# Attention's first scores behind its first gate's products, and the identity matrix on SyncE's queue

## The chip, the cores and the metric

One core of a Trainium2 chip runs the kernel. The metric is device time in microseconds (us) of one execution, the median of several. TensorE (PE in the profile) multiplies matrices; VectorE (DVE), ScalarE (ACT) and GpSimd (POOL) work element by element; SyncE (SP) issues DMAs, and so does ScalarE's queue here.

## The reference, cut to what matters

One decoder layer over 512 tokens of width 1024, in float32. A normalised input h is projected; one part of the columns goes through a gated linear recurrence (HGRN2, 8 heads), another through attention with low-rank queries and keys (MLA, 8 heads); both are gated, projected, merged and added to the input.

```python
h = rms_norm(x, norm_g[l])
proj = h @ w_in[l]
hq, hf, hi, hz, cq, ckv, kr, mz, glog = jnp.split(proj, pts, axis=-1)
y_a = hgrn2_branch(hq, hf, hi, hz, lower_bounds[l], hg_norm_g[l])
y_b = mla_branch(cq, ckv, kr, mz, q_a_g[l], w_uq[l], kv_a_g[l], w_ukv[l])
...
# in mla_branch, per block of 128 queries and per head:
s = (einsum(qn, k_nope) + einsum(qp, k_pe)) * scale      # nope part, rope part
p = softmax(where(causal, s, -inf))
out = p @ v                                              # then out * silu(mz)
```

## The kernel before

Every float32 product is made of three: each operand is split into a high and a low part (`w_hi`, `w_lo`, `hT0`, `hT1`), and `mm3` issues high x high, high x low and low x high (lines 90 to 92). Activations stand as 128 channels x 512 tokens. `load_w` (from line 94) brings a tile of weights of up to 128x1024 by SyncE's queue, casts it on ScalarE (L111) and subtracts on VectorE (L112). The pools for raw, high and low tiles hold three, four and four of them, so a cast waits until TensorE has used the tile four loads before. PSUM has eight banks: three for projections (`mm_ps`) and five for the rest (`ax_ps`), both used in rotation.

The stages: a start that normalises and transposes the four token tiles of x and makes the low-rank columns; then four pairs of HGRN2 heads (`hg_pair`); then the MLA heads 0 to 7; then the merge and the output projection. A scheduler sets the order on each engine by a time line of its own. It leaves alone what is written in a `manual_schedule` block, for the engines named there. There are three such blocks. The first is the start, by hand on TensorE, ScalarE and VectorE. The third is at the last MLA head. The second, `last_outputs`, is for TensorE alone: it is the seam between the last HGRN2 pair and the first MLA head. Instructions of other parts may still be put between those of the block, but theirs keep their order.

What stands in this second block:

- `outs(scores())`: the outputs of the last two HGRN2 heads (L508 to L529);
- `mla_scores(0, ...)`, from line 654: head 0's scores, for four blocks of 128 queries with 128, 256, 384 and 512 keys; per block three products of the nope part (`kn`, `qn`; L90 to L92) and two of the rope part (`kpe`, `qp`; L664). Softmax follows on VectorE (mask L667, maximum L668, scaling L669, reciprocal L671), ScalarE (exponential L670) and GpSimd (L672);
- `mla_gate(0)`, from line 644: 24 products of 512 columns with h (`hT`), then ScalarE (L548) and VectorE (L549);
- `gated(on)`: transposes of the HGRN2 outputs (L543), then VectorE (L544). These outputs, `k_2481` and `k_2502`, come from L535, for which ScalarE squares (L533) and GpSimd takes a power (L158, L159).

The rope operand `qp` has a long way: `mla_rope(0)` copies a projection on ScalarE (L605), moves its rows by DMAs on ScalarE's queue (L607), multiplies and adds on GpSimd (L608 to L610), moves rows again (L614), casts (L616, L619) and subtracts on VectorE (L620).

Behind the block come head 1's nope projections (`mla_nope(1)`, 15 products with `cT`), the values of heads 0 to 3 (`mla_values(0)`, 6 products for each of four token tiles), and the transposes of head 0's probabilities (L685).

At the start, SyncE's queue issues x's first token tile in two halves (L198), the first weights `c_raw[0]` (L201), x's second tile, the second weights, x's other tiles, then small rows and tables. ScalarE's queue issues a gain row (L204) and the identity matrix `ident` (L205, 64 KB). `ident` is the operand of all transposes, first of those of the first token tile (L253), from the normalised tile that VectorE makes (`xn`, L245). VectorE then casts the first weights (L232) and takes their low parts (L236), and TensorE multiplies (L264).

Of the kernel before, what the change touches and what calls it, by code (L numbers as in the profile page):

```python
# [38 lines left out]
def hybrid_layer(ctx: ExitStack, tc: tile.TileContext, a):  # L39
    nc = tc.nc  # L40
# [12 lines left out]
    def mm_tile():  # L53
        return mm.tile([P, 512], F32, tag="mm", name="mm_ps")

    def ax_tile():
        return ax.tile([P, 512], F32, tag="ax", name="ax_ps")

    def z_tile():
        return zpool.tile([P, S], F32, tag="z", name="z")  # L60
# [26 lines left out]
    def mm3(ps, l, r, lsl, rsl, start, stop):  # L87

        (lh, ll), (rh, rl) = l, r
        nc.tensor.matmul(ps, lh[lsl], rh[rsl], start=start, stop=False)  # L90
        nc.tensor.matmul(ps, lh[lsl], rl[rsl], start=False, stop=False)  # L91
        nc.tensor.matmul(ps, ll[lsl], rh[rsl], start=False, stop=stop)  # L92

    def load_w(*pieces, lo_eng=None):

        raw = wraw.tile([P, WCH], F32, tag="raw", name="w_raw")
        hi = whi.tile([P, WCH], F32R, tag="hi", name="w_hi")
        lo = wlo.tile([P, WCH], F32R, tag="lo", name="w_lo")
        views, o = [], 0
        for src in pieces:  # L100
            n = int(np.prod(src.shape[1:]))
            if len(src.shape) == 4:
                _, k, h, c = src.shape
                dst = raw[:, o : o + n].rearrange("p (k h c) -> p k h c", k=k, h=h)
                for i in range(k):
                    nc.sync.dma_start(dst[:, i], src[:, i])
            else:
                nc.sync.dma_start(raw[:, o : o + n].rearrange("p (k c) -> p k c", k=src.shape[1]), src)
            views.append([t[:, o : o + n].rearrange("p (k c) -> p k c", k=src.shape[1]) for t in (hi, lo)])
            o += n  # L110
        nc.scalar.copy(hi[:, :o], raw[:, :o])  # L111
        (lo_eng or nc.vector).tensor_tensor(lo[:, :o], raw[:, :o], hi[:, :o].bitcast(F32), op=ALU.subtract)  # L112
        return views[0] if len(views) == 1 else views
# [56 lines left out]
    ident = const.tile([P, P], F32, name="ident")  # L170
# [29 lines left out]
    def load_c(kh):  # L200
        nc.sync.dma_start(c_raw[kh][:].rearrange("p (k c) -> p k c", k=4), w_c0[:, 4 * kh : 4 * kh + 4, :])  # L201

    load_x(0, 2)
    nc.scalar.dma_start(ng_row[0:33:32, :], a["norm_g"].rearrange("l (n c) -> (l n) c", n=2))  # L204
    nc.scalar.dma_start(ident[:], a["c_ident"])  # L205
    load_c(0)
    load_x(1)
    load_c(1)
# [337 lines left out]
    def silu2(z, pz):  # L546

        nc.scalar.activation(z, pz, AF.Tanh, scale=0.5)  # L548
        nc.vector.scalar_tensor_tensor(z, z, 1.0, pz, op0=ALU.add, op1=ALU.mult)  # L549
# [3 lines left out]
    def hg_pair(pair, before_gate=None, last=None):  # L553
        cc, hs = pair * 256, (2 * pair, 2 * pair + 1)
        pf = proj_ch(w_in, COL_F + cc, hT)
        kk = [hg_forget(h, pf[i]) for i, h in enumerate(hs)]
        def gate():
            pz = proj_ch(w_in, COL_ZA + cc, hT)
            zz = [z_tile() for _ in hs]
            for i in range(2):  # L560
                silu2(zz[i][:], pz[i][:])
            return zz

        if pair % 2 == 0:
            for t in range(NT):
                v_sb[t] = hw.tile([P, 512], F32, f"v{t}")
            proj_tok(w_in, COL_I + cc, hT, lambda t, ps: nc.scalar.copy(v_sb[t][:], ps[:]))
        else:
            zz = gate()
        pq = proj_ch(w_in, COL_Q + cc, hT)  # L570
        qq = [hg_query(h, pq[i], kk[i][0]) for i, h in enumerate(hs)]
        sts = [hg_states(h, kk[i][5], kk[i][1], v_sb) for i, h in enumerate(hs)]
        if before_gate:
            before_gate()
        if pair % 2 == 0:
            zz = gate()
        def scores():
            return [hg_scores(h, kk[i][2], kk[i][3], kk[i][4], qq[i][0], qq[i][1]) for i, h in enumerate(hs)]

        def outs(aa):  # L580
            return [hg_out(h, aa[i], sts[i], qq[i][2], v_sb) for i, h in enumerate(hs)]

        def gated(on):
            for i, h in enumerate(hs):
                hg_gate(h, on[i], zz[i])

        if last:
            return last(scores, outs, gated)
        gated(outs(scores()))
# [54 lines left out]
    def mla_gate(h):  # L644
        w = load_w(w_in[:, COL_ZB + h * P : COL_ZB + h * P + P].rearrange("(k p) c -> p k c", p=P))
        ps = mm_tile()
        for k in range(KD):
            mm3(ps[:], w, hT, (slice(None), k), (slice(None), k), k == 0, k == KD - 1)
        z = z_tile()
        silu2(z[:], ps[:])  # L650
        return z


    def mla_scores(h, pool, qn, kn, qp, final=False):

        pn = []
        for i in range(NT):
            n = (i + 1) * P
            bl = slice(i * P, n)
            sps = ax_tile()  # L660
            qh = qp[h % 2]
            mm3(sps[:, :n], qn, kn, (slice(None), bl), (slice(None), slice(0, n)), True, False)
            for x in range(2):
                nc.tensor.matmul(sps[:, :n], qh[:, bl], kpe[x][:, :n], start=False, stop=x == 1)  # L664
            sm = pool.tile([P, 4], F32, "sm", 4)
            p = pool.tile([P, n], F32, f"p{i}")
            nc.vector.tensor_tensor(sps[:, bl], sps[:, bl], mask_inf[:], op=ALU.add)  # L667
            nc.vector.tensor_reduce(sm[:, 0:1], sps[:, :n], axis=AX.X, op=ALU.max, negate=True)  # L668
            nc.vector.tensor_scalar(sm[:, 1:2], sm[:, 0:1], SCALE, None, op0=ALU.mult)  # L669
            nc.scalar.activation(p[:, :n], sps[:, :n], AF.Exp, scale=SCALE, bias=sm[:, 1:2], accum_out=sm[:, 2:3])  # L670
            nc.vector.reciprocal(sm[:, 3:4], sm[:, 2:3])  # L671
            (nc.vector if final else nc.gpsimd).tensor_scalar(p[:, :n], p[:, :n], sm[:, 3:4], 0.5, op0=ALU.mult, op1=ALU.mult)  # L672
            pn.append(p)
        return pn
# [41 lines left out]
    def last_outputs(scores, outs, gated):  # L716

        with tc.manual_schedule(engines={mybir.EngineType.PE}):
            on = outs(scores())
            early.append(mla_scores(0, ma_pool, *early[1], early[0]))  # L720
            z = mla_gate(0)
            gated(on)
        return z

    z = hg_pair(H // 2 - 1, first_scores, last_outputs)
    hw.close()

# [5 lines left out]
    for h in range(H):  # L733
# [6 lines left out]
        if h:  # L740
            z = mla_gate(h)
# [144 lines left out]
```

## Time and profile before

| | |
|---|---|
| time, median of 3 runs | 636.34 us (635.45 to 636.77) |
| the profiled execution | 636.65 us, its span 634.9 us |
| TensorE busy | 622.2 us, 98% of the span |
| VectorE, ScalarE, GpSimd busy | 353.0, 239.7 and 114.5 us |
| mean granted clock of TensorE | 0.995 |
| moved by DMA | 59.75 MB, mean 94 GB/s |

How to read it: the span runs from the first instruction to the last; all times inside are from its start. A row of the timeline gives start, length, engine, line, operation, and what it writes and reads, and in brackets the idle time ahead of it and what ended that. The instructions of a busy engine start a little before the one ahead has ended in these rows, since matmuls are pipelined and their ends are modelled; starts are the better measure of what one costs in a row. The granted clock is the share of full speed that the chip lets TensorE run at. A busy share near 1 does not say that TensorE is at full speed: at half the clock it is busy too.

### The profile page before, as it was taken

The page shows a single profiled execution, that of the slowest core. Times are in us where ns is not written, and L with a number is a line of the kernel's source. Part 1 is how long each engine was busy: PE and PEld are TensorE (multiplying, and loading weights), DVE is VectorE, ACT ScalarE, POOL GpSimd, SP SyncE. Part 2 cuts the span into 40 slices and gives each one's busy share as a digit, 9 for nine tenths or more (in the row PEclk, how much of TensorE's full clock was granted, in tenths as well). Part 3 has the DMA queues.
Part 4 walks back from the last instruction along what each step waited for, and adds up shares of the span by engine and source line. Part 5 has one row for each costly group of instructions (what it writes and reads, how often), then busy time and mean ns, then how long its engine had stood idle before and what let it go on. Part 6 is the DMA issues. An engine that isn't in the chain of part 4 may idle for free.

```text
span 634.9 us, 8391 instructions
## 1 busy us (share of the span) xinstructions
PE 622.2 (98%) x3204; PEld 524.1 (83%) x3204; DVE 353.0 (56%) x552; ACT 239.7 (38%) x451; POOL 114.5 (18%) x213
## 2 busy tenths in 40 slices
PE   7999999999999999989999999999999999999995
PEld 4998888888888888878888888888888888888884
DVE  7727855397954458757366758584232342434244
ACT  5554242323233232356345546383222232323223
POOL 3106200322311033321314140000000010111011
PEclk9999999999999999989999999999999999999999
DMA  7425153124115203401532232223333323324403
GB/s 234 151 66 181 47 166 90 43 67 132 35 44 146 58 21 88 116 17 35 141 96 72 55 116 84 68 66 100 99 100 99 99 69 107 102 90 162 170 14 120
DMA packets 58808, 59.75 MB, mean 94 GB/s; under 512 B 5736, under 2 KB 52238, under 8 KB 58768
## 3 DMA queue, kind: packets, MB, share of 16 engines
q1 hardware_dynamic: 56492, 55.54, 29.0%
q10 hardware_dynamic: 2132, 3.15, 1.6%
q8 instruction: 25, 0.41, 0.3%
q0 software_dynamic: 144, 0.52, 0.2%
q14 instruction: 15, 0.12, 0.1%
HBM read 55.01 MB, written 2.10 MB: 90 GB/s over the span
## 4 chain that ended last, share of the span: by engine, by line
PE 94%; DMA 2%; DVE 1%; ACT 1%; POOL 1%; ACTq 0%; issue 0%; SPq 0%; POOLq 0%
PE mm_ps L90 26%; PE mm_ps L91 26%; PE mm_ps L92 26%; PE ax_ps L91 2%; PE ax_ps L90 2%; PE ax_ps L92 2%; PE ax_ps L664 2%; PE mm_ps L264 1%; PE ax_ps L685 1%; DMA w_raw<-w_in 1%; PE ax_ps L508 1%; PE ax_ps L527 1%; PE ax_ps L529 1%; PE ax_ps L496 1%; PE ax_ps L516 1%; PE ax_ps L543 1%
## 5 line engine op out<-in xcount | busy, mean ns | idle before, releaser
L112 DVE TENSOR_TENSOR w_lo<-w_raw,w_hi 128x1024 fp32r<-128x1024 f32 (+3 forms) x90 | 108.6, 1211 | 123.0 <-ACT w_hi L111 121.3
L111 ACT CAST w_hi<-w_raw 128x1024 fp32r<-128x1024 f32 (+3 forms) x90 | 89.4, 995 | 167.3 <-PE mm_ps L91 124.0
L90 PE MATMUL mm_ps<-hT,w_hi 128*128 128x512 f32 x384 | 150.8, 393 | 0.0
L91 PE MATMUL mm_ps<-hT,w_hi 128*128 128x512 f32 x384 | 150.0, 391 | 0.0
L92 PE MATMUL mm_ps<-hT,w_lo 128*128 128x512 f32 x384 | 149.8, 392 | 0.0
L92 PEld LDWEIGHTS mm_ps<-hT,w_lo 128*128 128x128 f32 x384 | 72.1, 188 | 14.7
L90 PEld LDWEIGHTS mm_ps<-hT,w_hi 128*128 128x128 f32 x384 | 72.1, 188 | 14.4
L91 PEld LDWEIGHTS mm_ps<-hT,w_hi 128*128 128x128 f32 x384 | 72.2, 188 | 14.3
L787 POOL TENSOR_TENSOR ma<-ma,z 128x512 f32<-128x512 f32 x8 | 11.8, 1479 | 177.1 <-DVE z L786 177.1
L91 PE MATMUL mm_ps<-w_lo,hT 128*128 128x512 f32 (+1 forms) x96 | 36.5, 382 | 0.0
L92 PE MATMUL mm_ps<-w_hi,hT 128*128 128x512 f32 (+1 forms) x96 | 36.4, 382 | 0.0
L90 PE MATMUL mm_ps<-w_hi,hT 128*128 128x512 f32 (+1 forms) x96 | 36.4, 386 | 0.0
L672 POOL TENSOR_SCALAR p<-p,sm 128x128 f32<-128x128 f32 (+3 forms) x28 | 15.3, 548 | 79.4 <-DVE sm L671 47.5
L453 DVE RECIPROCAL tf<-pr 128x512 f32<-128x512 f32 x8 | 26.8, 3350 | 0.2
L670 ACT ACTIVATE p<-ax_ps,sm 128x128 f32<-128x128 f32 (+3 forms) x32 | 16.9, 529 | 24.6 <-DVE sm L669 20.9
L91 PE MATMUL mm_ps<-ya,w_hi 128*128 128x512 f32 x64 | 25.0, 390 | 0.0
L92 PE MATMUL mm_ps<-ya,w_lo 128*128 128x512 f32 x64 | 24.9, 389 | 0.0
L90 PE MATMUL mm_ps<-yb,w_hi 128*128 128x512 f32 x64 | 24.9, 389 | 0.0
L91 PE MATMUL mm_ps<-yb,w_hi 128*128 128x512 f32 x64 | 24.9, 389 | 0.0
L92 PE MATMUL mm_ps<-yb,w_lo 128*128 128x512 f32 x64 | 24.9, 389 | 0.0
L90 PE MATMUL mm_ps<-ya,w_hi 128*128 128x512 f32 x64 | 24.8, 389 | 0.0
L154 DVE TENSOR_TENSOR wo<-wo_raw,wo 128x1024 fp32r<-128x1024 f32 x8 | 9.6, 1223 | 25.9 <-ACT wo L153 25.9
(226 smaller groups left out, 1126.3 us busy)
## 6 DMA issues: line engine op xcount, KB each, us to landing
w_raw<-w_in SPq DMA_DIRECT2D x58, 512.0 KB, 3.8
w_raw<-w_proj_a SPq DMA_DIRECT2D x8, 512.0 KB, 3.4
w_raw<-w_proj_b SPq DMA_DIRECT2D x8, 512.0 KB, 3.4
wo_raw<-w_out SPq DMA_DIRECT2D x8, 512.0 KB, 3.7
xr<-x SPq DMA_DIRECT2D x4, 512.0 KB, 7.2
w_raw<-w_in SPq DMA_DIRECT2D x4, 448.0 KB, 4.8
x<-x SPq DMA_DIRECT2D x3, 512.0 KB, 9.4
w_raw<-w_uq SPq DMA_DIRECT2D x8, 192.0 KB, 2.6
```

The source lines that it names most:

```text
L90: nc.tensor.matmul(ps, lh[lsl], rh[rsl], start=start, stop=False)
L91: nc.tensor.matmul(ps, lh[lsl], rl[rsl], start=False, stop=False)
L92: nc.tensor.matmul(ps, ll[lsl], rh[rsl], start=False, stop=stop)
L111: nc.scalar.copy(hi[:, :o], raw[:, :o])
L112: (lo_eng or nc.vector).tensor_tensor(lo[:, :o], raw[:, :o], hi[:, :o].bitcast(F32), op=ALU.subtract)
L154: nc.vector.tensor_tensor(lo, src, hi.bitcast(F32), op=ALU.subtract)
L264: nc.tensor.matmul(ps, hT[l][:, 4 * kh + k, t * P : t * P + P], c_hl[kh][r][:, k * 256 : k * 256 + 256], start=kh == 0 and kind == 0 and k ...
L453: nc.vector.reciprocal(rp[:], pr[:])
L664: nc.tensor.matmul(sps[:, :n], qh[:, bl], kpe[x][:, :n], start=False, stop=x == 1)
L670: nc.scalar.activation(p[:, :n], sps[:, :n], AF.Exp, scale=SCALE, bias=sm[:, 1:2], accum_out=sm[:, 2:3])
L672: (nc.vector if final else nc.gpsimd).tensor_scalar(p[:, :n], p[:, :n], sm[:, 3:4], 0.5, op0=ALU.mult, op1=ALU.mult)
L787: nc.gpsimd.tensor_tensor(ma[:, j], ma[:, j], g[:], op=ALU.add)
```

## The change

Two edits.

```diff
     load_x(0, 2)
     nc.scalar.dma_start(ng_row[0:33:32, :], a["norm_g"].rearrange("l (n c) -> (l n) c", n=2))
-    nc.scalar.dma_start(ident[:], a["c_ident"])
+    nc.sync.dma_start(ident[:], a["c_ident"])
     load_c(0)
...
         with tc.manual_schedule(engines={mybir.EngineType.PE}):
             on = outs(scores())
+            z = mla_gate(0)
             early.append(mla_scores(0, ma_pool, *early[1], early[0]))
-            z = mla_gate(0)
             gated(on)
```

The identity's DMA goes from ScalarE's queue, where it stood behind the gain row and ahead of the load of the activation table, to SyncE's, behind the halves of x's first tile and ahead of the first weights. In the block, head 0's gate comes ahead of its scores. The instructions are the same in number. The scheduler then sets the order of all that it is free to order anew, on TensorE, VectorE, ScalarE and GpSimd up to the last MLA head.

On TensorE at the seam, behind the last HGRN2 output (L529), before. The buffers `kn_2430` and `qn_2419` are head 0's, `qp_2394` its rope operand:

```order
L529 MATMUL ax_ps<-st,q_2330 128x128
L90 MATMUL ax_ps<-kn_2430,qn_2419 128x128
L91 MATMUL ax_ps<-kn_2431,qn_2419 128x128
L92 MATMUL ax_ps<-kn_2430,qn_2420 128x128
L664 MATMUL ax_ps<-kpe_91,qp_2394 128x128
L664 MATMUL ax_ps<-kpe_92,qp_2394 128x128
L90 MATMUL ax_ps<-kn_2430,qn_2419 128x256
```

And after, from the gate's last product on (23 more stand between it and the same L529); `cT` is head 1's nope projection:

```order
L92 MATMUL mm_ps<-hT_123,w_lo 128x512
L90 MATMUL ax_ps<-kn_2430,qn_2419 128x128
L91 MATMUL ax_ps<-kn_2431,qn_2419 128x128
L92 MATMUL ax_ps<-kn_2430,qn_2420 128x128
L90 MATMUL mm_ps<-cT_89,w_hi 128x512
L664 MATMUL ax_ps<-kpe_91,qp_2394 128x128
L664 MATMUL ax_ps<-kpe_92,qp_2394 128x128
L90 MATMUL ax_ps<-kn_2430,qn_2419 128x256
```

All 24 gate products, and one of head 1's, moved ahead of the first product that reads `qp_2394`.

On VectorE at the same place, behind the two L620 that make head 0's rope operand, before:

```order
L620 TENSOR_TENSOR qp_2395<-qs,qh 64x512
L667 TENSOR_TENSOR ax_ps<-ax_ps,mask_inf 128x128
L668 TENSOR_REDUCE sm<-ax_ps 128x1
L667 TENSOR_TENSOR ax_ps<-ax_ps,mask_inf 128x128
L669 TENSOR_SCALAR sm<-sm 128x1
L535 TENSOR_TENSOR k_2481<-ax_ps,ss 128x512
L668 TENSOR_REDUCE sm<-ax_ps 128x1
L671 RECIPROCAL sm<-sm 128x1
```

And after:

```order
L620 TENSOR_TENSOR qp_2395<-qs,qh 64x512
L535 TENSOR_TENSOR k_2481<-ax_ps,ss 128x512
L535 TENSOR_TENSOR k_2502<-ax_ps,ss 128x512
L667 TENSOR_TENSOR ax_ps<-ax_ps,mask_inf 128x128
L112 TENSOR_TENSOR w_lo<-w_raw,w_hi 128x1024
L668 TENSOR_REDUCE sm<-ax_ps 128x1
L667 TENSOR_TENSOR ax_ps<-ax_ps,mask_inf 128x128
L549 SCALAR_TENSOR_TENSOR z<-z,mm_ps 128x512
L667 TENSOR_TENSOR ax_ps<-ax_ps,mask_inf 128x128
L669 TENSOR_SCALAR sm<-sm 128x1
L668 TENSOR_REDUCE sm<-ax_ps 128x1
```

Head 0's softmax now stands behind both L535, and in the midst of a weight tile's split (L112) and the gate's pass (L549), which used to follow it. Before, the whole softmax came ahead of that L112. ScalarE's queue has the cast of the 1024 columns and L548 ahead of the four exponentials (L670) now, and the cast of 640 columns, L153 of `qn` and `kn` still behind them.

## The prediction

> **What bounds the kernel now.** I read the page first (span, busy shares, granted clock), then TensorE's list of waits, then the timeline around the longest of them, then the granted clock in short windows.
>
> ```profile
> span 634.9 us, 8391 instructions
> ...
> PE 622.2 (98%) x3204; PEld 524.1 (83%) x3204; DVE 353.0 (56%) x552; ACT 239.7 (38%) x451; POOL 114.5 (18%) x213
> ...
> PEclk9999999999999999989999999999999999999999
> ```
>
> TensorE is idle for 634.9 - 622.2 = 12.7 us in all, and its clock is full but for one slice in the middle. An edit pays where TensorE stands still or runs slowly, and nowhere else. Its list of waits has seven entries; these three concern the change.
>
> ```profile
> PE ax_ps L664 <- DVE qp L620: 2.2, 1, 2.2
> ...
> PE ax_ps L253 <- DMA ident<-c_ident: 0.8, 1, 0.8
> PE mm_ps L264 <- DVE w_lo L236: 0.6, 1, 0.6
> ```
>
> The longest, and the only one of the seven behind the first 20 us, lies inside the block that the change reorders. TensorE's timeline (start, length, instruction) shows it, and how the following work runs:
>
> ```profile
> 270.57 0.30 PE L90 MATMUL ax_ps<-kn,qn 128*128 128x128 f32 x1
> ...
> 273.32 0.44 PE L664 MATMUL ax_ps<-kpe,qp 128*128 128x128 f32 x2 [2.22 <-DVE qp L620]
> ...
> 277.81 0.39 PE L90 MATMUL mm_ps<-hT,w_hi 128*128 128x512 f32 x1
> ...
> 283.25 1.03 PE L543 MATMUL ax_ps<-ident,k 128*128 128x128 f32 x8
> 284.04 0.48 PE L90 MATMUL mm_ps<-cT,w_hi 128*128 128x512 f32 x1
> ...
> 287.55 1.25 PE L685 MATMUL ax_ps<-ident,p 128*128 128x128 f32 x10
> 288.56 0.48 PE L90 MATMUL mm_ps<-w_hi,cT 128*128 128x512 f32 x1
> ...
> 293.00 0.22 PE L91 MATMUL ax_ps<-kn,qn 128*128 128x128 f32 x1
> ...
> 293.92 0.34 PE L90 MATMUL ax_ps<-kn,qn 128*128 128x384 f32 x1
> ...
> 294.79 0.39 PE L90 MATMUL ax_ps<-kn,qn 128*128 128x512 f32 x1
> ```
>
> Head 0's scores take from 270.57 to 277.81, 7.24 us. The clock (third figure from the end) says why that is more than the wait:
>
> ```profile
> 272.00:274.00 2.00, 0.68 (x5) 0.68 (x6) 1.39 (x3) 1.90 (x9) 0.30 (x1) 0.94 0.00 0
> 274.00:276.00 2.00, 2.00 (x9) 2.00 (x9) 1.64 (x6) 1.57 (x9) 1.70 (x4) 0.50 0.00 0
> 276.00:278.00 2.00, 2.00 (x8) 1.69 (x7) 1.84 (x8) 0.56 (x2) 0.95 (x2) 0.70 0.01 4
> ```
>
> Right behind the wait the clock is halved. What is lost is 2 x (0.06 + 0.50 + 0.30) = 1.72 us of full-speed time.
>
> **The scores behind the gate.** First, what the scores cost undisturbed. Head 1's show it: its eight small products from 293.00 to 293.92 stand 0.115 us apart, its five of 384 columns take 0.87, and products of 512 columns stand (283.25 - 277.81) / 24 = 0.227 apart. Ten small, five of 384, five of 512: 1.15 + 0.87 + 1.13 = 3.15 us. So 7.24 - 3.15 = **4.09 us** come back if the wait and the slow clock both go: 2.37 of wait and 1.72 of clock.
>
> Will they go? The operand that comes last, and the weights of the gate, which now must be there at 270.57:
>
> ```profile
> 259.66 1.21 DVE L112 TENSOR_TENSOR w_lo<-w_raw,w_hi 128x1024 fp32r<-128x1024 f32 x1
> ...
> 272.58 1.40 DVE L620 TENSOR_TENSOR qp<-qs,qh 64x512 fp32r<-64x512 f32 x2 [4.32 <-ACT qh L616]
> ```
>
> The split at 259.66 is that of gate 0's weights (by the order), done 9.7 us ahead. The gate then covers 270.57 to 276.01 (24 x 0.227 = 5.44). The rope operand (first of the two L620) is there at 273.3. ScalarE and VectorE stand in the same order up to it, so it doesn't move, and 2.7 us of cover are left.
>
> What is late next? Softmax of head 0 used to run on VectorE while TensorE did the gate; now the gate's own work on VectorE comes at the same time. In the new order VectorE has, behind the second L535: 16 softmax steps, the splits of the next two weight tiles (1024 and 640 columns) in between, and four 128x512 passes (L549, two L544, L154 of qn). TensorE waits for the last of these, which frees the bank of head 1's qn for the second tile of values. The rows for their lengths (the first four are groups: count, busy, mean ns; the others single):
>
> ```profile
> L668 DVE TENSOR_REDUCE sm<-ax_ps 128x1 f32<-128x128 f32 (+3 forms) x8 | 3.8, 483 | 0.0
> ...
> L667 DVE TENSOR_TENSOR ax_ps<-ax_ps,mask_inf 128x128 f32<-128x128 f32 x8 | 2.4, 296 | 1.7 <-PE ax_ps L664 1.7
> ...
> L671 DVE RECIPROCAL sm<-sm 128x1 f32<-128x1 f32 x7 | 1.1, 158 | 1.9 <-ACT p L670 1.9
> L669 DVE TENSOR_SCALAR sm<-sm 128x1 f32<-128x1 f32 x8 | 1.1, 148 | 0.0
> ```
> ```profile
> 285.21 1.22 DVE L112 TENSOR_TENSOR w_lo<-w_raw,w_hi 128x1024 fp32r<-128x1024 f32 x1
> 286.35 0.68 DVE L549 SCALAR_TENSOR_TENSOR z<-z,mm_ps 128x512 f32<-128x512 f32 x1
> 287.00 0.69 DVE L154 TENSOR_TENSOR qn<-mm_ps,qn 128x512 fp32r<-128x512 f32 x1
> ```
> ```profile
> 275.58 1.01 POOL L159 TENSOR_TENSOR ss<-ss,fixed 128x4 f32<-128x4 f32 x1
> ```
> ```profile
> 279.77 0.69 ACT L670 ACTIVATE p<-ax_ps,sm 128x512 f32<-128x512 f32 x1 [1.01 <-DVE sm L669]
> ...
> 287.51 0.73 ACT L111 CAST w_hi<-w_raw 128x640 fp32r<-128x640 f32 x1 [0.55 <-PE mm_ps L91]
> ```
>
> Steps in a row start 0.03 to 0.08 closer than their lengths (285.21 to 286.35 is 1.14, then 0.65). Softmax: 4 x (0.483 + 0.296 + 0.158 + 0.148) = 4.34, less 16 x 0.06, is 3.4; splits 1.14 + 0.72; passes 4 x 0.65 = 2.6; together 7.9. The start is fixed by GpSimd at 276.6, and one L535 pass makes it 277.2. Without any wait VectorE would be through at 285.1. It does wait: block 3's maximum comes to its turn last and is scaled at about 282.9; the exponentials of blocks 2 and 3 follow each other on ScalarE to about 284.25 (0.7 and 0.8 with their reads); the cast of the 640 columns stands behind them there (0.73, to 285.0), then the split on VectorE (0.72), L544 and L154 (0.65 each): 287.0.
>
> TensorE gets to that tile at 270.57 + 5.44 + 3.15, then as in the rows above the eight transposes L543 (0.79), head 1's 15 products (3.51), the first values tile (6 x 0.227 = 1.36), ten transposes L685 (1.01), and two first products of head 1's scores (0.23): 286.06. So it waits about **0.9 us**, in pieces. Ends: 0 (VectorE through at 285.1), and with whole lengths (9.3 in place of 7.9) 288.4, so 2.4. I take 0.9, the walk with starts, since starts are what these rows show.
>
> The scheduler has also rewritten the order of the later heads on four engines. No instruction is added, and TensorE has no wait there before; I take 0, with an end of +0.5.
>
> **The identity.** The rows at the start (the first from the chain of waits, the others from the timeline):
>
> ```profile
> 1.62 7.11 DMA w_raw<-w_in
> ```
> ```profile
> 1.62 0.48 SPq L201 DMA_DIRECT2D w_raw<-w_in  x1
> ...
> 1.90 0.36 ACTq L205 DMA_DIRECT2D ident<-c_ident  x1
> ...
> 8.05 1.07 PE L253 MATMUL ax_ps<-ident,xn 128*128 128x128 f32 x8 [0.82 <-DMA ident<-c_ident]
> ...
> 8.75 0.76 DVE L232 CAST w_hi<-w_raw 128x512 fp32r<-128x512 f32 x2 [0.34 <-DMA w_raw<-w_in]
> ```
>
> The transposes may start up to 0.3 us sooner. But the chain that ends last doesn't run through them: it runs through the first weights' load (issued at 1.62, landed at 8.73), then VectorE's casts and splits, for which TensorE waits at L264. So the gain is hidden. The cost: on SP's queue this load, and all behind it, is issued one issue later, 0.36 to 0.48. That is its upper end if the load's landing follows its issue. The lower end is -0.3, if the load gains what the identity's 64 KB took of the DMA engines on the other queue: 64 KB at the 234 GB/s of the page's first slice.
>
> ```profile
> GB/s 234 151 66 181 47 166 90 43 67 132 35 44 146 58 21 88 116 17 35 141 96 72 55 116 84 68 66 100 99 100 99 99 69 107 102 90 162 170 14 120
> ```
>
> In between lies a load that lands 7.1 us after its issue, set by what is queued before it rather than by its issue: I take **+0.1**. ScalarE loses an issue of 0.36 ahead of its table load; its first square then waits for x in any case, worth 0.
>
> **Sum.** -4.1 + 0.9 + 0.1 = -3.1 us. The profiled execution took 636.65 (1.75 around its span); that is 0.31 over the median of 636.34, to which I apply the sum: **633.2 us**.
>
> **Rivals.** Something under 0.2% (1.3 us) can't be told from no change here.
> (a) No new wait: ScalarE and VectorE keep ahead. 636.34 - 4.09 + 0.1 = 632.3. For it: 285.1 against 286.06. Against: the order puts the exponentials before the cast.
> (b) The slow clock isn't the wait's doing and stays. Then only 2.37 returns: 636.34 - 2.37 + 0.9 + 0.1 = 635.0. Against: the three windows, halved just behind the wait, in the only slice of the page that is not full. [...]
> (c) The new wait, too, halves the clock: one of 1.0 to 2.4 us plus 1.72. At 1.7 us: 636.34 - 4.09 + 1.7 + 1.72 + 0.1 = 635.8. Against: its pieces are short, with products in between.
> (d) The reordered heads lose what is won here: 636.3, no change.
> (e) Slower: the splits that now stand between the mask and the maxima on VectorE are slow. One took far longer than its size:
>
> ```profile
> 264.94 1.53 DVE L112 TENSOR_TENSOR w_lo<-w_raw,w_hi 128x384 fp32r<-128x384 f32 x1
> ```
>
> That is 384 columns in 1.53, where 285.21 has 1024 in 1.22 (0.46 by size): 3.3 times. On this chain's 1.86 us of splits it would add 4.3, a wait of 5.2 and the slow clock: 636.34 - 4.09 + 5.2 + 1.72 + 0.1 = 639.3. It decides from a wait of 2.4 us up (4.09 - 1.72). Against: GpSimd multiplied during that row, and has only short rescalings here.
>
> **How the numbers follow.** Forecast 0.60 (new wait 0.3 to 1.9: 632.6 to 634.2, and up to +0.5 at the start and +0.5 later), (a) 0.17, (b) 0.06, (c) 0.09, (d) 0.04, (e) 0.04. From 632.0 (case (a) with the identity's -0.3) to 635.2 (the forecast's upper ends, and (b)) the range holds 0.83. Faster by over 0.2% is under 635.1: 0.60 + 0.17 + 0.06 and 0.02 of (c), 0.85; slower 0.04; the rest, 0.11, within.
>
> **What the profile after would show.** Right: no wait of L664 for qp; gate products from 270.6 (shifted by the start); scores in 3.2 us at clock 1.0; a wait of the order of 1 us of TensorE for ScalarE or VectorE (kn, qn) near 286; the wait for the identity gone, and TensorE's L264 still waiting for w_lo. Wrong: a clock under 1.0 near 274 or near 288; a wait over 2 us there; a new wait in heads 2 to 7; L232 later than 9.2.

## The result and the profile after

| | before | after |
|---|---|---|
| median | 636.42 us (635.45 to 636.77, 4 runs) | 632.95 us (632.74 to 633.21, 4 runs) |
| the profiled execution | 636.65, span 634.9 | 633.0, span 631.2 |

The ratio is 0.9948, with an interval of 0.9931 to 0.9965: 3.5 us less. In later runs, beside the experiments, the change took 633.0 (5 runs) against 636.23 (15 runs): 0.9951, 0.9938 to 0.9963.

From the page after: TensorE's idle time in the span falls from 12.7 to 9.4 us, and the slice with the lower clock is gone.

```profile
span 631.2 us, 8391 instructions
...
PE 621.8 (99%) x3204; PEld 523.4 (83%) x3204; DVE 353.5 (56%) x552; ACT 239.6 (38%) x451; POOL 115.1 (18%) x213
...
PEclk9999999999999999999999999999999999999999
```

TensorE's list of waits behind 20 us is down to one entry, a new one. The wait for `qp` and, at the start, the one for `ident` are gone.

```profile
PE mm_ps L90 <- DVE qn L154: 0.2, 1, 0.2
```

TensorE's timeline after: the gate runs from 270.21, the scores from 275.77 to 279.18.

```profile
270.21 0.48 PE L90 MATMUL mm_ps<-hT,w_hi 128*128 128x512 f32 x1
...
275.77 0.22 PE L90 MATMUL ax_ps<-kn,qn 128*128 128x128 f32 x1
...
276.33 0.33 PE L664 MATMUL ax_ps<-kpe,qp 128*128 128x128 f32 x2
...
279.18 0.60 PE L543 MATMUL ax_ps<-ident,k 128*128 128x128 f32 x4
...
284.18 0.60 PE L543 MATMUL ax_ps<-ident,k 128*128 128x128 f32 x4
284.62 1.26 PE L685 MATMUL ax_ps<-ident,p 128*128 128x128 f32 x10
285.63 0.48 PE L90 MATMUL ax_ps<-kn,qn 128*128 128x128 f32 x2
286.30 0.50 PE L90 MATMUL mm_ps<-w_hi,cT 128*128 128x512 f32 x1 [0.20 <-DVE qn L154]
...
289.15 0.22 PE L91 MATMUL ax_ps<-kn,qn 128*128 128x128 f32 x1
```

The scores take 3.41, of which 0.23 is the one product of head 1 that slipped in: 3.18, where before took 7.24. **4.06 us** are gone. Before the second values tile there is a gap: the products at 285.63 take 0.23, the next starts at 286.30, so **0.44** between starts are the new wait (the list shows 0.20 of it). The whole stretch from the end of the HGRN2 outputs to L91 took 270.57 to 293.00, 22.43; now 270.21 to 289.15, 18.94. That is 3.49 less, 0.13 short of 4.06 - 0.44; another 0.36 came at the start, and 0.2 was lost again on the way to the end, since the profiled executions differ by 3.65.

The clock over the scores and the gap is full (columns: length, TensorE busy with its count, granted clock, DMA share, GB/s):

```profile
276.00:278.00 2.00, 2.00 (x15) 1.00 0.01 4
...
284.00:286.00 2.00, 2.00 (x18) 1.00 0.05 8
286.00:288.00 2.00, 1.80 (x8) 1.00 0.30 64
```

### The profile page after: what moved, and what is told of

It reads as the page before. It is cut to its first block, busy times and chain, and to the rows that moved or that the text cites. A ratio compares the mean times of both kernels' runs of the same rounds, so it can differ in the third digit from the quotient of the medians.

```text
span 631.2 us, 8391 instructions
## 1 busy us (share of the span) xinstructions
PE 621.8 (99%) x3204; PEld 523.4 (83%) x3204; DVE 353.5 (56%) x552; ACT 239.6 (38%) x451; POOL 115.1 (18%) x213
## 4 chain that ended last, share of the span: by engine, by line
PE 93%; DVE 2%; ACT 2%; POOL 1%; issue 1%; DMA 0%; ACTq 0%; POOLq 0%
PE mm_ps L90 25%; PE mm_ps L92 25%; PE mm_ps L91 25%; PE ax_ps L92 2%; PE ax_ps L91 2%; PE ax_ps L90 2%; PE mm_ps L264 1%; PE ax_ps L664 1%; PE ax_ps L685 1%; PE ax_ps L508 1%; PE ax_ps L229 1%; PE ax_ps L527 1%; PE ax_ps L529 1%; PE ax_ps L496 1%; PE ax_ps L516 1%
## 5 line engine op out<-in xcount | busy, mean ns | idle before, releaser
L112 DVE TENSOR_TENSOR w_lo<-w_raw,w_hi 128x1024 fp32r<-128x1024 f32 (+3 forms) x90 | 109.1, 1216 | 131.5 <-ACT w_hi L111 130.2
L91 PE MATMUL mm_ps<-hT,w_hi 128*128 128x512 f32 x384 | 149.8, 390 | 0.0
L91 PEld LDWEIGHTS mm_ps<-hT,w_hi 128*128 128x128 f32 x384 | 72.2, 188 | 14.4
L91 PE MATMUL mm_ps<-w_lo,hT 128*128 128x512 f32 (+1 forms) x96 | 36.5, 382 | 0.0
L672 POOL TENSOR_SCALAR p<-p,sm 128x128 f32<-128x128 f32 (+3 forms) x28 | 16.9, 606 | 72.9 <-DVE sm L669 59.5
L670 ACT ACTIVATE p<-ax_ps,sm 128x128 f32<-128x128 f32 (+3 forms) x32 | 16.9, 529 | 25.0 <-DVE sm L669 24.9
L91 PE MATMUL mm_ps<-ya,w_hi 128*128 128x512 f32 x64 | 25.0, 390 | 0.0
L91 PE MATMUL mm_ps<-yb,w_hi 128*128 128x512 f32 x64 | 24.9, 389 | 0.0
```

## The experiments

### The two parts by themselves

`seam_only` has only the second edit. It ran twice, the second time (`seam_again`) beside the unchanged change (`after_again`). `ident_only` has only the first edit.

> Only the seam: the gate ahead of the scores, the identity stays on ScalarE's queue. If the earlier start in the trace after (everything 0.37 to 0.40 us earlier from 10 us on) comes from the identity's move, this kernel gains the seam's part alone: 3.1 to 3.4 us, and the seam's first product starts near 270.6 as before. If the prediction's term for the identity (+0.1, a loss) is right and the early start in the one trace was chance, it is as fast as the whole change or 0.1 faster: a gain of 3.5.

> The seam alone once more, as the partner of the whole change: 633.0 to 633.2 if the identity's move brings nothing, 633.4 if it brings 0.4, 632.9 if it costs 0.1.

> The change as it is, beside its parts on the same chip. It contains no long wait of TensorE, so its times should stand within 0.5 us of each other, and small terms can be told. If the identity's move brings nothing, it is equal to the seam alone to 0.15 us; if the move brings what the one trace suggested, it is 0.4 faster; by the prediction's term 0.1 slower.

> Only the identity's move. Theory that the move frees the first weights' landing: 0.4 us faster than before, VectorE's L232 near 8.36 without a wait for the load, the scores at 270.2, and behind it the same 2.2 us wait at L664 or one 0.4 longer, since the rope operand may not come earlier. The prediction's term: 0.1 slower (at most 0.48), L232 at 8.75 to 9.2. Chance: within 0.1.

| | median us | range | runs | ratio to before |
|---|---|---|---|---|
| seam_only | 633.1 | 632.94 to 633.35 | 5 | 0.9955 (0.9941 to 0.9969) |
| seam_again | 632.95 | 632.68 to 633.06 | 5 | 0.9950 (0.9937 to 0.9962) |
| after_again | 633.0 | 632.88 to 633.1 | 5 | 0.9951 (0.9938 to 0.9963) |
| ident_only | 635.52 | 635.36 to 636.87 | 11 | 0.9997 (0.9987 to 1.0006) |

The seam is the whole gain. The identity's move is worth nothing that can be seen: 633.0 with it and 632.95 without, on one chip. The median of `ident_only` is lower than before's beside it (636.15) only because 6 of its 11 executions fall in the faster of two groups (next section), where before has 25 of 57; the ratio is 0.9997. Why then did the trace after start 0.36 earlier? VectorE's cast of the first weights, in `seam_only` (identity on ScalarE's queue), then `ident_only`:

```profile
8.46 0.76 DVE L232 CAST w_hi<-w_raw 128x512 fp32r<-128x512 f32 x2
```
```profile
8.49 0.76 DVE L232 CAST w_hi<-w_raw 128x512 fp32r<-128x512 f32 x2
```

Both stand at 8.5, behind VectorE's own work and no longer behind a load. It was before's one execution that came late (8.75, waiting for the weights): in nine other traces, with either place of the identity, L232 starts 1.32 or 1.33 behind VectorE's `xn` (L245) and does not wait for the load; in before, 1.75 behind. The wait for the identity is as little a fixed price of ScalarE's queue: of eight traces with the identity there, only before (0.82) and `long_wait` (0.7, described below) list it. The identity late, behind the first weights, says the same:

```diff
-    nc.scalar.dma_start(ident[:], a["c_ident"])
     load_c(0)
+    nc.sync.dma_start(ident[:], a["c_ident"])
```

> Before's seam, and the identity on SyncE's queue behind the first weights instead of ahead of them, so that the weights are issued at 1.62 as before. If what helps is that ScalarE's queue no longer carries the identity, this gains as much as the identity's move alone, or 0.1 to 0.4 more, unless the transposes now wait for the identity. If what helps is the place ahead of the weights, it gains nothing, and the first weights land near 8.7. By the prediction (issue sets landing, to a part) it is 0 to 0.1 faster than before.

It took 636.43 (635.51 to 636.6, 11 runs), ratio 1.0001 (0.9992 to 1.0010), its L232 at 8.46. Queue and place both leave the time alone.

### The wait and the clock

The profile of `ident_only` was a surprise. It has before's seam and before's wait, and its clock is full throughout:

```profile
270.29 0.30 PE L90 MATMUL ax_ps<-kn,qn 128*128 128x128 f32 x1
...
272.96 0.44 PE L664 MATMUL ax_ps<-kpe,qp 128*128 128x128 f32 x2 [2.14 <-DVE qp L620]
...
274.40 0.51 PE L664 MATMUL ax_ps<-kpe,qp 128*128 128x384 f32 x2
275.25 0.50 PE L90 MATMUL ax_ps<-kn,qn 128*128 128x512 f32 x1 [0.34 <-ACT p L670]
...
276.49 0.39 PE L90 MATMUL mm_ps<-hT,w_hi 128*128 128x512 f32 x1
```
```profile
272.00:274.00 2.00, 1.04 (x8) 1.00 0.00 0
274.00:276.00 2.00, 1.66 (x9) 1.00 0.01 4
```

So the halved clock does not always follow the wait. And without it the scores still take 6.20 (270.29 to 276.49), since at full speed they run into the softmax: the first product of 512 columns waits for an exponential. The halved clock costs 7.24 - 6.20 = 1.04, not 1.72. The times show the same two cases. Of the 57 executions of before beside the three sets of experiments, 25 took 635.14 to 635.71 (median 635.48, mean clock 0.997 or 0.998) and 32 took 636.10 to 637.81 (median 636.44, 0.993 to 0.996), with none between: 0.96 apart. (The mean clock also counts what stands behind the last product, where a lower clock costs nothing: from 628 us on it is 0.80 in before and 0.51 in the trace after, and `filler6`, below, has 0.64 from 627 us on and 0.996 over its profile, with 1.00 over the scores.)

Does the wait make the clock fall? Products whose result nothing uses were put ahead of the scores, to fill it:

```diff
+            for _ in range(fill if i == 0 else 0):
+                nc.tensor.matmul(sps[:, P:], qn[0][:, :P], kn[0][:, P:], start=True, stop=True)
             mm3(sps[:, :n], qn, kn, ...)
```

with `fill` 12, 6 and 3, for head 0 alone; all else as before. (The added lines make L664 into L666 and L670 into L672 in these kernels.)

> Before's order, with 12 products of 384 columns (about 0.17 us each, 2.0 together) put ahead of head 0's first scores; their result is not used by anything. They fill most of the wait for the rope operand, which still comes at 273.3. If the halved clock comes from that wait (the prediction), the 1.72 us return though the products still wait for the operand: 634.7, and the granted clock is 1.0 from 272 to 278. If the slow clock is not the wait's doing (rival b), the time stays 636.4 and the clock is halved near 275 as before.

> Before's order with only 6 unused products of 384 columns ahead of head 0's first scores (1.0 us), so that TensorE still waits about 1.2 us for the rope operand. The runs so far: with the whole wait of 2.2 us about half of the executions show the lower clock and take 636.2 to 637.8, the others 635.3 to 635.7; with the wait filled (12 products) none of 11 does. [...] Theory that any wait can do it, with a chance that goes with its length: a quarter of the executions above 636.1.

> Before's order with 3 unused products (0.5 us) ahead of head 0's scores, so that about 1.7 us of the wait are left. With 2.2 us left 34 of 64 executions showed the lower clock, with 1.2 none of 11. [...] Theory of a chance in proportion to the wait: 4 of 11.

| wait of L664 in the profile | executions above 636.0 | median below, above | ratio to before |
|---|---|---|---|
| 2.1 to 2.2 (before, ident_only, ident_late) | 44 of 79 | before: 635.48, 636.44 | |
| 1.6 (filler3) | 5 of 11 | 635.49, 636.57 | 0.9998 (0.9989 to 1.0006) |
| 1.2 (filler6) | 0 of 11 | 635.52, none | 0.9994 (0.9985 to 1.0003) |
| none (filler12) | 0 of 11 | 635.50, none | 0.9993 (0.9984 to 1.0002) |

With the wait filled the slower case is gone: at a chance of 0.56, none of 11 happens about once in 8,000. The clock falls because TensorE stands still, at 1.6 and 2.2 us in about half of the executions. At 1.2 us none of 11 showed it, which still leaves room for a chance below about a quarter, so whether there is a limit stays open. The proportion is unlikely: a quarter would give none of 11 about once in 24. And `filler12`, expected at 634.7, took 635.5: it has the full clock, and the wait for the exponential (0.33) that the slow clock used to hide.

In the windows of `filler3`, whose profile caught a halving, then of `long_wait`:

```profile
272.00:274.00 2.00, 1.11 (x6) 0.79 0.00 0
274.00:276.00 2.00, 2.00 (x9) 0.50 0.01 4
276.00:278.00 2.00, 2.00 (x9) 0.86 0.00 0
```
```profile
270.00:272.00 2.00, 0.00 (x0) 0.70 0.37 85
272.00:274.00 2.00, 1.25 (x6) 0.50 0.01 4
274.00:276.00 2.00, 2.00 (x8) 0.50 0.00 0
276.00:278.00 2.00, 2.00 (x7) 0.59 0.00 0
```

`long_wait` makes the wait longer, by the scores ahead of the HGRN2 outputs:

```diff
-            on = outs(scores())
+            aa = scores()
             early.append(mla_scores(0, ma_pool, *early[1], early[0]))
+            on = outs(aa)
             z = mla_gate(0)
```

> Head 0's scores, in before's order, also ahead of the 14 products that make the last HGRN2 outputs (128 columns, 1.6 us together), so that TensorE stands at the rope operand from 1.6 us earlier: a wait of about 3.8 us in place of 2.2. The 1.6 us of work come later, so an undisturbed execution takes about 637.1, more if the HGRN2 outputs come late then. [...] Theory that it is chance and has nothing to do with the length: half, as before.

The wait became 5.4 us, more than the 3.8 expected, since the outputs are 3.0 us of work. All 5 executions show the low clock (0.993) and take 639.97 to 640.83; ratio 1.0069 (1.0056 to 1.0081). The run speaks against a chance that has nothing to do with the length, but five executions are few: at 0.56 all five would be slow about once in 18. Time at half clock, from the windows: before 2 x (0.06 + 0.50 + 0.30) / 0.5 = 3.44 us, `filler3` 3.40, `long_wait` 6.84, twice as long. By the mean clock of the window in which it begins (0.94, 0.79 and 0.70, where a whole window at half clock has 0.50), the half clock starts at 273.8 in before, 273.2 in `filler3` and 270.8 in `long_wait`: 2.7, 1.9 and 3.4 us behind the beginning of the wait, and in `long_wait` 2.0 ahead of its end. So it keeps no fixed distance from the wait, and a wait of 1.64 us was enough. Why one execution halves and the next does not is not shown.

### The new wait

`gated_first` moves `gated(on)` ahead of the scores too, with both edits of the change in:

```diff
             z = mla_gate(0)
-            early.append(mla_scores(0, ma_pool, *early[1], early[0]))
             gated(on)
+            early.append(mla_scores(0, ma_pool, *early[1], early[0]))
```

> The change, with the transposes of the HGRN2 outputs ahead of the scores as well; the scheduler puts head 1's 15 products with cT ahead of them. qn's split on VectorE now stands ahead of most of the softmax. If the new wait is the softmax chain ahead of qn's split, it goes, and the time is 632.6. If instead the softmax now comes late for the transposes of the probabilities (L685), TensorE waits there: 633.5 or more.

> The change with the transposes of the HGRN2 outputs ahead of the scores, once more, beside the change itself. If its 632.63 came from the missing wait for qn (0.36 to 0.40 us between starts in the traces of the change), it is 0.3 to 0.4 faster than the change here too. If it was the chip or the hour, the two are equal.

It took 632.63 (632.57 to 632.89) and, beside the change, 632.7 (632.64 to 632.86) against 633.0 (632.88 to 633.1): each of its five runs there is below each of the change's five. Ratios to before: 0.9949 (0.9937 to 0.9962) and 0.9947 (0.9934 to 0.9961). TensorE has no wait left behind 20 us. The transposes start at 288.68 without one:

```profile
288.44 0.39 PE L92 MATMUL mm_ps<-w_hi,cT 128*128 128x512 f32 x1
288.68 0.81 PE L685 MATMUL ax_ps<-ident,p 128*128 128x128 f32 x6
289.25 0.31 PE L90 MATMUL ax_ps<-kn,qn 128*128 128x128 f32 x1
```

So 0.3 of the 0.44 could be had. It is faster than both kernels.

`gate_split` puts the scores behind 6 of the gate's 24 products (identity as before):

```diff
-    def mla_gate(h):
+    def mla_gate(h, between=None):
         ...
         for k in range(KD):
+            if between and k == 2:
+                between()
```

> Six of the 24 gate products ahead of head 0's scores, 18 behind. The scheduler has put head 1's 15 products with cT between the first three scores and the first that reads the rope operand, so 21 large products (4.8 us) cover 2.4 us. The softmax and qn's split both start earlier against TensorE's work, the gate's pass on VectorE later. If the new wait of the change (0.4 us in the trace after) is VectorE's queue ahead of qn, it goes: 632.6. If the gate's late pass then holds up the transposes' passes and the banks, it is 633 or above. With the identity on ScalarE's queue, as before.

It took 633.7 (633.52 to 633.99), ratio 0.9966 (0.9952 to 0.9979), no better than the change (0.9951). The wait for `qn` went, and two others came, as the second theory had it:

```profile
PE ax_ps L90 <- DVE ya L544: 0.3, 1, 0.3
PE mm_ps L90 <- DVE z L549: 0.2, 1, 0.2
```

## Why the prediction was right, and where its steps were not

The forecast was 633.2, the time is 632.95 to 633.0; the mechanism is the one that it named. By its steps:

**The wait and the scores.** 4.09 was to come back, and 4.06 came in the profiled execution: no wait of L664, 3.18 for the scores, a full clock. But the term took 1.72 of slow clock as the wait's certain consequence. The runs show that it is the wait's doing, in 44 of 79 executions, and that its net price is 0.96 to 1.04, since the softmax is late next when the clock is full. Against the executions of before that kept their clock the change gains 2.5 (635.48 to 633.0), against the others 3.4. The rows say the same: 6.20 in `ident_only` less 3.18 is 3.02, less the new wait 2.6. The sum of -3.1 came out near by luck, because the profiled execution and the first median (636.34) were both of the second kind; against the first kind it is 0.6 too large. Rival (b), that the slow clock stays, is wrong, though in 35 of the 79 executions the wait passed without it.

**The new wait.** 0.9 was forecast, 0.44 measured. The place, the engine and the operand were right. VectorE's walk was too slow by 0.4: moved forward by the 0.36 of the start, it was to be through at 286.6 and was at 286.24. ScalarE's and VectorE's rows after:

```profile
282.56 0.68 ACT L670 ACTIVATE p<-ax_ps,sm 128x512 f32<-128x512 f32 x1
...
283.22 0.72 ACT L111 CAST w_hi<-w_raw 128x640 fp32r<-128x640 f32 x1
```
```profile
283.98 1.01 DVE L112 TENSOR_TENSOR w_lo<-w_raw,w_hi 128x640 fp32r<-128x640 f32 x1 [0.45 <-ACT w_hi L111]
284.91 0.74 DVE L544 SCALAR_TENSOR_TENSOR ya<-ax_ps,hg_half,z 128x512 f32<-128x512 f32 x1
285.57 0.67 DVE L154 TENSOR_TENSOR qn<-mm_ps,qn 128x512 fp32r<-128x512 f32 x1
```

The exponentials were done earlier: the cast starts at 283.22, where the walk, so moved, had 283.9. The split behind it was slower, 0.93 between starts where 0.72 was taken. TensorE came to the tile at 285.86, 0.16 later than the forecast's 286.06 moved likewise (285.70). On this term rival (a), no new wait, is as near as the forecast; (c) fell, since a gap of 0.44 left the clock at 1.00. Rival (e) needed splits 3.3 times slower; the one of 640 columns took 1.01, where 1.22 for 1024 gives 0.76 by size. The traces point to GpSimd, which (e) had named: in the trace after this split takes 1.01, and begins while GpSimd rescales probabilities (L672, 282.95 to 284.32); in before it takes 0.83 (at 288.27) and another of 640 columns 0.82 (at 256.34), and GpSimd does nothing just then. The forecast took these rescalings as too short to matter; beside them the split is 0.2 longer. No experiment takes them away by itself, so this cause is not shown.

**The later heads.** Taken as 0: no wait stands there, and 0.2 of the profiled gain is lost over the last 340 us, within the 0.5 allowed; it was not taken apart. Rival (d) fell.

**The identity.** Taken as +0.1, measured as none to 0.1 (633.0 against 632.95). That the first weights' load would land later by part of its later issue was wrong: in `ident_only` VectorE does not wait for it. The step that failed is the reading that this load sets VectorE's start; that held in before's one trace alone (8.75), and in the nine others VectorE's own work sets it. The wait for the identity did go in the trace after, but it is absent from most traces with the identity on ScalarE's queue too, and its going is no gain.

## What to carry to other kernels

A wait of TensorE can cost more than the list shows: it may halve the clock (here from 1.6 us on), in some executions and not in others, and both the wait and what the slow clock hides must be read before a gain is put on it. If a kernel's times fall into two groups, compare the clocks of the two before a trace of one of them is taken as the kernel. Start times that differ by 0.4 us between two single traces are no evidence on an edit: run each edit alone.

## What the runs showed of the hardware

- TensorE's granted clock halved for 3.40 to 3.44 us behind some waits of 1.64 and 2.22 us, and for 6.84 at one of 5.4, from ahead of its end. By the times, waits of 1.2 did it in none of 11 executions and those of 5.4 in all of 5.
- Between starts a wait costs more than the list of waits shows: in `ident_only` the listed 0.34 stands for 275.25 - 274.40 - 2 x 0.17 = 0.51, in the trace after the listed 0.20 for 0.44. The list counts from the end of the row ahead, and the next product starts ahead of that end where nothing is waited for (in the trace after, at 278.02 behind a row of 277.68 + 0.51). The product after the one that waited starts 0.33 later in both, where 0.23 is usual; but 0.32 also stands there without a wait (270.21 to 270.53 in the trace after), so that the wait alone does this is not shown.
- VectorE's split of 640 columns took 1.01 us in the trace after, where GpSimd worked as it began, and 0.82 and 0.83 in before, where it did not.
- The first weights' load let VectorE start at 8.49 when issued at 2.15 (`ident_only`), and at 8.75, still waited for, when issued at 1.62 (before). In five other traces (`seam_only`, `seam_again`, `ident_late`, `filler12`, `filler3`) it was issued at 1.62 to 1.64 and VectorE started at 8.21 to 8.46 without a wait. So the 0.5 us between the two issues did not decide when VectorE could start.
